# One transpose or two for the queries and keys of a pair of blocks

## The chip, the cores and the metric

The kernel runs on one core of a Trainium2 chip. A core has five engines that run side by side: TensorE for matrix products (PE in the profile; the loading of its weights is listed apart as PEld), VectorE (DVE), ScalarE (ACT), GpSimd (POOL) and SyncE (SP). SP computes nothing here: it issues the transfers, one after another in the order of the program, and 16 DMA engines carry them out. The metric is the time of one execution on the device, in microseconds (us). Three executions of the kernel before took 1917.46, 1920.43 and 1922.58 us, so the median is 1920.43 us.

## The reference

The program is one layer of an encoder block on 2048 positions of width 1024. All of it must come out, in float32:

```python
h = rms_norm(x, norm_gain)
qa, ka, va, qb, kb, vb, ga, gb, mg = split(h @ w_in)          # one combined projection
# mixer A: 8 query heads, 2 key heads, window of 128 positions to each side, a sink logit per head
ya = banded_attention(norm(qa) / 8, norm(ka), va, 128, 1, rel_bias[:, :8], sink_a) * silu(ga)
# mixer B: three groups of 8 heads, (window, dilation) = (128, 1), (512, 4), (2048, 16)
for g: o_g, lse_g = dilated_group(norm(qb_g) / 8, norm(kb_g), vb_g, window_g, dilation_g, bias_g)
yb = sum_g softmax_g(lse)_g * o_g * silu(gb)
out = x + (sigmoid(mg_a) * (ya @ w_branch_a) + sigmoid(mg_b) * (yb @ w_branch_b)) @ w_out
```

The products are made with operands that are split into a high and a low half-precision part, so each float32 product is three half-precision products on TensorE.

## The kernel before, in words

**Stages.** First x is normed, transposed and split (`XH`, `XL`) and a gate is projected. Then come 14 *units*, each a few heads of one mixer: `A` twice and `B` twelve times (four head pairs by three dilations). The first unit is A, the second B with dilation 4, the third A again, and the rest are B. After the units come the merge gates, the branch projections and the output projection, which this change does not touch.

**A unit** walks over 16 blocks of 128 positions, two at a time: a *pair*, eight pairs to a unit. For each block TensorE projects q, k and v into PSUM (`matmuls`, L695). Then, for the whole pair, ACT copies q and k out (`rw`), ACT, DVE and POOL norm and scale them, ACT and DVE write the high and the low part into a tile `spl` (`hi`, L768, and `lo`, L772), and POOL copies the keys once more with the two parts exchanged (`swap`, L777, one copy for each block). `spl` so holds, for each of the two blocks, six strips of 128 columns. In a unit of kind A five heads are normed together for each block (four query heads and one key head, plus the exchanged key); in kind B four (two and two, plus two exchanged).

**The transposes.** The scores need q and k with the head's elements on the partitions, so SP issues a DMA transpose from `spl` into a tile `kq` (`turn`, L785). Before, that is one transpose per block, six strips of 128 by 128, into a tile of its own. There are six such tiles used in turn, and three more (`kq0`) for block 0 of units of kind B that need it again at their end.

**An item** is one block of queries and two heads. An A pair makes four items. Each has score products on TensorE (`logits`, L845, which read `kq`), a minimum with the bias on DVE (L860), exponentials on ACT (L868), the split into `p` (ACT L873, DVE L877), a DMA transpose of `p` into `pt` (`turn` of the item, L883), and the products with v on TensorE (`values`, L894, which read `pt`). In an A unit a `pt` transpose moves twelve strips of 128 by 128 (eight at the unit's ends). The four `pt` tiles are used in turn.

**What sets the order.** The program's order on each engine is written out by hand: each step of a pair or item is put into a heap with a time in units of a pair's length (`NORM`, `LAGS`, `LV`), and the heap is emptied in order of that time between TensorE's products. The times only set an order. On the chip an instruction starts when its engine reaches it and the semaphores that it waits for have come. SP therefore carries, in one queue, the `kq` and `pt` transposes, the loads of weights (`wraw`, L176), biases (`b`, L669) and gate values (`yo`, L944), and the stores (`ytd`, L975, and `zd`, L929).

Of the kernel before, what the change touches and what calls it, by code (L numbers as in the profile page):

```python
# [22 lines left out]
F16 = mybir.dt.float16  # L23
# [9 lines left out]
NT = S // 128  # L33
# [63 lines left out]
X_US = dict(look=0.25, land=4.3, next=1.45, late=.12, sq=1.14, st=.17, ln=.2, nw=.75, sc=1.24, tr=.8, hi=.5, lo=.62, gs=2.1, pw=1.3,  # L97
            gh=1.06, gl=1.26, mm=.217, th=.6, gt=.63, us=.83, uh=.75, ul=.82, ag=1.0, tl=1.3)
XT_BUFS = 14
KQ_BUFS = 6  # L100
VT_BUFS = 10
PT_BUFS = 4
N_BIAS_A = 384
# [3 lines left out]
def block_kernel(tc, x, w_units, w_gate, w_mrg, w_out, w_bra, w_brk, gain, qkg, sink, bias_a, bias_b, b_merge, out):  # L107
    nc = tc.nc
    V = nc.vector
    A = nc.scalar  # L110
# [511 lines left out]
    wk = main.enter_context(tc.tile_pool(name="wk", bufs=2, reuse_waits="tile"))  # L622
# [55 lines left out]
    class Pair:  # L678
# [98 lines left out]
                G.tensor_copy(sp[:, i, nh:, :, :], sp[:, i, nq:nh, ::-1, :])  # L777

        def turn(self):
            for i, s in enumerate(self.subsets):  # L780
                if self.un.shift and s[1] == 0:
                    kq = wk.tile([128, 6, 128], F16, name="kq0", bufs=3)
                else:
                    kq = wk.tile([128, 6, 128], F16, name="kq", bufs=KQ_BUFS)
                nc.sync.dma_start_transpose(out=kq[:], in_=self.sp[:, i].rearrange("p a b c -> p (a b c)"))  # L785
                self.un.kq[s] = kq


    class Item:
# [1215 lines left out]
    outs = [Out(s) for s in range(8)]  # L2005
# [14 lines left out]
    for s in range(8):  # L2020
        p = pos[0]
# [92 lines left out]
```

## Time and profile before

| | |
|---|---|
| median of 3 executions | 1920.43 us |
| the profiled execution | 1923.34 us, of which the span of its instructions is 1920.9 us |
| TensorE busy | 1876.6 us, 98% of the span |
| VectorE busy | 1501.5 us, 78% |
| ScalarE busy | 1251.2 us, 65% |
| DMA transposes | 224 of `kq`, 256 of `pt`, all issued by SP |
| granted TensorE clock, mean | 0.998 |

A row of the waits reads: the engine and line that waited, what it waited for, the sum of the waits, how many, and the longest. In a timeline a row gives start, duration, engine, line, operation, tiles written and read, count, and in brackets the idle time just ahead of it with what ended it. A row of windows gives the stretch, its length, the busy time of each engine with its count of instructions, the granted clock, the share of the DMA engines' time and the bytes moved. SP's rows are the time that the issuing takes; the packets of a transfer move later.

In the profiled execution the first unit A has its pairs between some 95 and 231 us, the second between some 288 and 425 us.

### The profile page before, as it was taken

Reading aid. Unit: us, or ns where it says so; the run is one execution under the profiler, and the core shown is the slowest. Engines: PE = TensorE matmul, PEld = TensorE weight load, DVE = VectorE, ACT = ScalarE, POOL = GpSimd, SP = SyncE. Lnnn points to the kernel's source line nnn. Section 1 sums busy time; section 2 is a strip of 40 time slices with the busy share of each in tenths; the row PEclk is TensorE's granted clock in tenths of the full one; section 3 lists DMA queues with packets and bytes.
Section 4 is the critical chain, followed back from the end, with each engine's and each line's share of the span. In section 5 each row is a group of like instructions: output and inputs, shape, how many; then the busy total and the mean of one; then the engine's idle time right before and its main releaser. Section 6 shows DMA issues by size and latency. Waiting matters only on the chain.

```text
span 1920.9 us, 51094 instructions
## 1 busy us (share of the span) xinstructions
PE 1876.6 (98%) x19242; PEld 1439.4 (75%) x19242; DVE 1501.5 (78%) x3835; ACT 1251.2 (65%) x3015; POOL 579.1 (30%) x1363
## 2 busy tenths in 40 slices
PE   6999999999999999999999999999999999899998
PEld 4568987789999899988999898544444446676774
DVE  7679878986887889878789888657778644977885
ACT  8477768887777777777767766575675865433441
POOL 1034333443553435543455445200000001222121
PEclk9999999999999999999999999999999999999999
DMA  6259998988888679887888777776576557854551
GB/s 255 83 98 197 165 183 143 190 169 165 166 150 182 138 156 202 153 157 175 146 169 160 137 148 146 180 295 181 182 214 181 183 186 252 270 153 120 148 153 61
DMA packets 639351, 326.21 MB, mean 170 GB/s; under 512 B 459264, under 2 KB 589952, under 8 KB 636672
## 3 DMA queue, kind: packets, MB, share of 16 engines
q1 hardware_dynamic: 638960, 322.70, 72.6%
q8 instruction: 150, 2.46, 0.6%
q14 instruction: 97, 0.79, 0.2%
q10 hardware_dynamic: 144, 0.26, 0.0%
HBM read 139.08 MB, written 73.66 MB: 111 GB/s over the span
## 4 chain that ended last, share of the span: by engine, by line
PE 86%; DMA 6%; DVE 4%; ACT 2%; issue 1%; SPq 1%; POOL 0%; DVEq 0%; POOLq 0%
PE pj L695 42%; PE fps L1600 17%; PE fps L1984 7%; PE fps L1912 6%; PE s L845 5%; PE pv L894 4%; DMA pt<-p 2%; PE pj L350 2%; PE pj L302 1%; PE fps L302 1%; DMA kq<-spl 1%; DMA bigl<-ytd 1%; PE pt L958 1%; DMA bigl<-sd 1%; PE s L480 0%
## 5 line engine op out<-in xcount | busy, mean ns | idle before, releaser
L695 PE MATMUL pj<-wl,XH 128*128 128x128 f16 (+2 forms) x2816 | 715.9, 268 | 0.0
L695 PE MATMUL pj<-wh,XL 128*128 128x128 f16 (+2 forms) x2816 | 712.2, 269 | 0.0
L695 PE MATMUL pj<-wh,XH 128*128 128x128 f16 (+2 forms) x2816 | 709.4, 268 | 0.0
L695 PEld LDWEIGHTS <-XH 128*128 128x128 f16 x5632 | 575.4, 112 | 54.6
L695 PEld LDWEIGHTS <-XL 128*128 128x128 f16 x2816 | 316.0, 112 | 24.0
L860 DVE CUSTOM_DVE_ANT_0 pr<-s,b,ubuf 128x256 f32<-128x256 f32 (+3 forms) x512 | 218.9, 465 | 42.1 <-PE s L845 39.5
L877 DVE SCALAR_TENSOR_TENSOR p<-pr,p 128x512 f16<-128x512 f32 (+2 forms) x256 | 195.8, 765 | 51.5 <-ACT p L873 48.6
L762 POOL TENSOR_TENSOR rw<-rw,g 128x128 f32<-128x128 f32 (+1 forms) x224 | 149.2, 686 | 202.5 <-DVE rw L755 170.2
L1922 POOL TENSOR_TENSOR g<-g,t 128x512 f32<-128x512 f32 x32 | 48.5, 1515 | 529.5 <-DVE t L1845 529.5
L1600 PEld LDWEIGHTS <-wh 128*128 128x128 f16 x1064 | 104.2, 99 | 123.5 <-issue 0.6
L713 ACT ACTIVATE rw<-pj 128x256 f32<-128x256 f32 (+1 forms) x224 | 87.4, 390 | 130.0 <-PE pj L695 129.3
L777 POOL COPY spl<-spl 128x256 f16<-128x256 f16 (+1 forms) x224 | 96.7, 461 | 244.5 <-DVE spl L772 244.5
L873 ACT ACTIVATE p<-pr 128x512 f16<-128x512 f32 (+2 forms) x256 | 157.7, 616 | 14.6 <-DMA pt<-p 10.3
L1912 PE MATMUL fps<-y,bigh 128*128 128x128 f16 x1792 | 153.8, 219 | 3.9 <-DVE r L1845 3.9
L1984 PE MATMUL fps<-WO,mf 128*128 128x512 f16 x672 | 151.9, 382 | 3.8 <-DVE xr L1991 3.8
L1912 PE MATMUL fps<-y,bigl 128*128 128x128 f16 x896 | 151.8, 219 | 0.0
L845 PE MATMUL s<-kq 128*128 128x128 f16 (+1 forms) x1856 | 148.2, 218 | 3.6 <-DMA kq<-spl 2.7
L1912 PEld LDWEIGHTS <-bigh 128*128 128x128 f16 x1792 | 139.1, 98 | 11.6 <-issue 4.3
L845 PEld LDWEIGHTS <-kq 128*128 128x128 f16 x2016 | 130.9, 98 | 19.9 <-issue 4.5
L894 PE MATMUL pv<-vt,pt 128*128 128x65 f16 (+1 forms) x2784 | 131.9, 193 | 8.1 <-DMA pt<-p 7.4
L894 PEld LDWEIGHTS <-pt 128*128 128x128 f16 x3024 | 119.3, 98 | 24.1 <-DMA pt<-p 12.1
L768 ACT ACTIVATE spl<-rw 128x512 f16<-128x512 f32 (+1 forms) x112 | 72.0, 643 | 80.3 <-POOL vt L724 70.2
(252 smaller groups left out, 3816.7 us busy)
## 6 DMA issues: line engine op xcount, KB each, us to landing
wraw<-in_w_units_dram SPq DMA_DIRECT2D x56, 384.0 KB, 4.8
g<-mgd SPq DMA_DIRECT2D x64, 256.0 KB, 4.9
wraw<-in_w_mrg_dram SPq DMA_DIRECT2D x45, 256.0 KB, 4.2
mgd<-t SPq DMA_DIRECT2D x43, 256.0 KB, 2.9
zd<-z SPq DMA_DIRECT2D x128, 66.0 KB, 2.0
zz<-zd SPq DMA_DIRECT2D x64, 132.0 KB, 3.4
xt<-in_x_dram SPq DMA_DIRECT2D x16, 512.0 KB, 8.2
ytd<-yo SPq DMA_DIRECT2D x32, 256.0 KB, 3.3
```

The source lines that it names most:

```text
L695: out.append(lambda lhs=lhs, rhs=rhs, ch=ch, a=a, b=b, k=k: T.matmul(ps[:, a:b], lhsT=lhs[:, ch, :], rhs=rhs[:, ch, a:b], start=(k == 0), ...
L713: A.activation(self.rw[:, n * i:n * i + n], self.ps[i][:, :n], AF.Copy)
L762: G.tensor_tensor(q[:, i, :un.nq, :], q[:, i, :un.nq, :], g, OP.mult)
L777: G.tensor_copy(sp[:, i, nh:, :, :], sp[:, i, nq:nh, ::-1, :])
L845: T.matmul(self.sv[j][:, o:o + k1 - k0], lhsT=q[:, h, :], rhs=kt[:, un.nq + kh + v * un.nk, k0:k1], start=(v == 0), stop=(v == 1))
L860: V.tensor_tensor_reduce(out=self.pv[:, j, self.p0:self.p0 + W], in0=self.sv[j], in1=un.bias[:, self.h0 + j, self.b0:self.b0 + W], scale=I ...
L873: A.activation(self.sp[:, :128 * n], self.pr, AF.Copy, scale=PSC)
L877: V.scalar_tensor_tensor(self.sp[:, 128 * n:], self.pr, PSC, self.sp[:, :128 * n], OP.mult, OP.subtract)
L894: T.matmul(self.po[:, j, :w], lhsT=p[:, n * j + s, :], rhs=un.v[key][:, vh, c0:c0 + w], start=(k == 0 and s == 0), stop=(k == 2 and s == n ...
L1600: T.matmul(b[k][:], lhsT=w[:, i, ch, :], rhs=xform(PROD[i][0], lo, ch, q), start=(i < 3 and n == 0), stop=(n == 11), skip_group_check=True)
L1912: out.append(lambda p=p, c=c, wl=wl, yl=yl, n=n: T.matmul(ps[:, 128 * p:128 * p + 128], lhsT=w[wl][:, i, c, p, :], rhs=y[:, yl, c, :], sta ...
L1984: out.append(lambda p=p, ml=ml, wl=wl, k=k: T.matmul(ps[:], lhsT=m[:, ml, p, :], rhs=WO[:, i, wl, p, :], start=(fresh and k == 0), stop=(k ...
```

## The change

For units of kind A the two blocks of a pair are transposed by one DMA transpose of twelve strips into one pair tile of `[128, 12, 128]`. For units of kind B there are still two transposes of six strips, now into the two halves of a pair tile. Four pair tiles are used in turn, in the place of six block tiles. `kq0` stays only for block 0 of a B unit of 16 blocks in a row (dilation 1), in one tile in the place of three; with dilation 4 block 0 stays in its pair tile. The room is the same: nine blocks' worth of tiles before and after.

```diff
@@ -97,7 +97,7 @@
 XT_BUFS = 14
-KQ_BUFS = 6
+KQ_BUFS = 4
 VT_BUFS = 10
@@ -777,13 +777,16 @@
         def turn(self):
+            kq = wk.tile([128, 12, 128], F16, name="kq", bufs=KQ_BUFS)
+            outs = [kq[:, 6 * i:6 * i + 6] for i in range(2)]
+            if self.un.shift and self.un.n == NT and self.subsets[0][1] == 0:
+                outs[0] = wk.tile([128, 6, 128], F16, name="kq0", bufs=1)[:]
+            if self.un.kind == "A":
+                nc.sync.dma_start_transpose(out=kq[:], in_=self.sp[:].rearrange("p s a b c -> p (s a b c)"))
             for i, s in enumerate(self.subsets):
-                if self.un.shift and s[1] == 0:
-                    kq = wk.tile([128, 6, 128], F16, name="kq0", bufs=3)
-                else:
-                    kq = wk.tile([128, 6, 128], F16, name="kq", bufs=KQ_BUFS)
-                nc.sync.dma_start_transpose(out=kq[:], in_=self.sp[:, i].rearrange("p a b c -> p (a b c)"))
-                self.un.kq[s] = kq
+                if self.un.kind == "B":
+                    nc.sync.dma_start_transpose(out=outs[i], in_=self.sp[:, i].rearrange("p a b c -> p (a b c)"))
+                self.un.kq[s] = outs[i]
```

Every line after the function stands three lines lower in the changed kernel: L845 becomes L848, L883 becomes L886.

The order of the instructions on TensorE, VectorE, ScalarE and GpSimd is the same, instruction by instruction. On SP 16 transposes are gone, one for each of the 16 pairs of the two A units, and nothing else has moved past another.

SP's queue in the first unit A, seventh and eighth pair, before. In brackets is what a row waits for: `DMAHW` and a number is the completion of an earlier transfer, `Pool`, `DVE` and `PE` are the engines.

```order
L785 DMA_TRANSPOSE kq<-spl 128x6x128 [waits DMAHW1_49,Pool_49]
L785 DMA_TRANSPOSE kq<-spl 128x6x128 [waits DMAHW2_49,Pool_49]
L944 DMA yo<-gtd_88 128x512 [waits DMAHW3_49]
L883 DMA_TRANSPOSE pt_2417<-p_2357 128x12x128 [waits DMAHW4_49,DVE_49,PE_49]
L975 DMA ytd<-yo 128x512 [waits DMAHW5_49,DVE_49]
L883 DMA_TRANSPOSE pt_2496<-p_2445 128x12x128 [waits DMAHW6_49,DVE_49,PE_49]
L176 DMA wraw<-in_w_units_dram 128x768 [waits DMAHW7_49]
L176 DMA wraw<-in_w_units_dram 128x768 [waits DMAHW0_49]
L883 DMA_TRANSPOSE pt_2581<-p_2533 128x12x128 [waits DMAHW1_49,DVE_49,PE_49]
L883 DMA_TRANSPOSE pt_2664<-p_2616 128x12x128 [waits DMAHW2_49,DVE_49,PE_49]
L785 DMA_TRANSPOSE kq<-spl 128x6x128 [waits DMAHW3_49,Pool_49]
L785 DMA_TRANSPOSE kq<-spl 128x6x128 [waits DMAHW4_49,Pool_49]
```

The same place in the changed kernel:

```order
L785 DMA_TRANSPOSE kq<-spl 128x12x128 [waits DMAHW3_49,Pool_49]
L947 DMA yo<-gtd_88 128x512 [waits DMAHW4_49]
L886 DMA_TRANSPOSE pt_2403<-p_2345 128x12x128 [waits DMAHW5_49,DVE_49,PE_49]
L978 DMA ytd<-yo 128x512 [waits DMAHW6_49,DVE_49]
L886 DMA_TRANSPOSE pt_2482<-p_2431 128x12x128 [waits DMAHW7_49,DVE_49,PE_49]
L176 DMA wraw<-in_w_units_dram 128x768 [waits DMAHW0_49]
L176 DMA wraw<-in_w_units_dram 128x768 [waits DMAHW1_49]
L886 DMA_TRANSPOSE pt_2567<-p_2519 128x12x128 [waits DMAHW2_49,DVE_49,PE_49]
L886 DMA_TRANSPOSE pt_2650<-p_2602 128x12x128 [waits DMAHW3_49,DVE_49,PE_49]
L785 DMA_TRANSPOSE kq<-spl 128x12x128 [waits DMAHW4_49,Pool_49]
```

Each `pt` transpose and each load behind a pair's q and k stands one transpose nearer to the front. The single transpose waits for POOL's second copy (`swap`) of its pair, where the first of two waited for the first copy alone.

TensorE in the first unit A, before: scores of the item that is the first to read the second block of a pair, the rows where the wait for that block's own transpose stands.

```order
L845 LDWEIGHTS kq
L845 MATMUL s<-kq 128x128 [waits DMAHW2_49]
L845 LDWEIGHTS kq
L845 MATMUL s<-kq 128x128
L845 LDWEIGHTS kq
L845 MATMUL s<-kq 128x128 [waits DVE_49]
```

The same rows in the changed kernel:

```order
L848 LDWEIGHTS kq
L848 MATMUL s<-kq 128x128
L848 LDWEIGHTS kq
L848 MATMUL s<-kq 128x128
L848 LDWEIGHTS kq
L848 MATMUL s<-kq 128x128 [waits DVE_49]
```

The wait for the second block has gone; the item before, the first to read the pair's first block, waits for the one transpose that brings both. In the units of kind B the waits for `kq` and for its tiles to come free are for the same instructions as before.

## The prediction

> **What bounds the kernel.** I read the page's first lines and its chain of waits first.
>
> ```profile
> span 1920.9 us, 51094 instructions
> PE 1876.6 (98%) x19242; PEld 1439.4 (75%) x19242; DVE 1501.5 (78%) x3835; ACT 1251.2 (65%) x3015; POOL 579.1 (30%) x1363
> ...
> PE 86%; DMA 6%; DVE 4%; ACT 2%; issue 1%; SPq 1%; POOL 0%; DVEq 0%; POOLq 0%
> ```
>
> TensorE is busy 98% of the span and the change takes no work from it. What can be won is idle time of TensorE, and only where a transfer in the two A units ends that idle time. So the second view is that of windows: the steady part of the first and of the second A unit, then all B units behind them, then two stretches for the clock, then four for the transfers.
>
> ```profile
> 134.00:231.00 97.00, 90.84 (x1349) 80.10 (x1345) 84.64 (x220) 76.62 (x182) 36.30 (x80) 0.98 1.04 185
> 308.00:425.00 117.00, 114.82 (x1410) 95.27 (x1407) 107.32 (x279) 101.07 (x244) 49.64 (x103) 1.00 0.94 170
> 425.00:1230.00 805.00, 802.28 (x9720) 739.74 (x9719) 666.63 (x2016) 572.22 (x1601) 370.58 (x991) 1.00 0.82 161
> 202.00:204.00 2.00, 2.00 (x26) 1.73 (x26) 1.21 (x4) 1.80 (x4) 0.00 (x0) 0.54 1.19 266
> 204.00:206.00 2.00, 2.00 (x14) 1.45 (x12) 0.76 (x3) 1.98 (x6) 0.00 (x0) 0.61 0.74 147
> ...
> 176.00:179.90 3.90, 3.90 (x63) 3.89 (x61) 3.73 (x16) 3.06 (x6) 1.43 (x2) 1.00 1.17 285
> 179.90:181.50 1.60, 0.73 (x8) 0.47 (x5) 1.60 (x3) 0.08 (x1) 1.43 (x1) 1.00 1.37 51
> 199.60:201.60 2.00, 0.16 (x3) 0.00 (x0) 1.04 (x4) 0.42 (x2) 0.85 (x5) 1.00 1.35 84
> 341.50:343.00 1.50, 1.30 (x16) 0.85 (x14) 1.36 (x4) 0.63 (x2) 0.86 (x1) 1.00 1.47 32
> ```
>
> TensorE idles 97.0 - 90.84 = 6.2 us in the first A unit, 117.0 - 114.82 = 2.2 us in the second, and 2.7 us in 805 us of B. In A the DMA engines' share is 0.94 to 1.04 (over 1 is possible, packets overlap): they have hardly any room. The last three rows show transfers that nearly stop for 1.5 to 2 us (32 to 84 GB/s, against 285 GB/s just before). The third view is TensorE's timeline at its waits:
>
> ```profile
> 141.36 0.32 PE L894 MATMUL pv<-vt,pt 128*128 128x65 f16 x5 [0.73 <-DMA pt<-p]
> 182.71 0.35 PE L894 MATMUL pv<-vt,pt 128*128 128x65 f16 x6 [2.08 <-DMA pt<-p]
> 196.42 0.36 PE L894 MATMUL pv<-vt,pt 128*128 128x65 f16 x6 [0.36 <-DMA pt<-p]
> 201.90 0.38 PE L894 MATMUL pv<-vt,pt 128*128 128x65 f16 x7 [2.14 <-DMA pt<-p]
> 343.56 0.32 PE L894 MATMUL pv<-vt,pt 128*128 128x65 f16 x5 [0.76 <-DMA pt<-p]
> 373.84 0.30 PE L894 MATMUL pv<-vt,pt 128*128 128x65 f16 x4 [0.56 <-DMA pt<-p]
> 384.39 0.29 PE L894 MATMUL pv<-vt,pt 128*128 128x65 f16 x4 [0.76 <-DMA pt<-p]
> ...
> PE s L845 <- DMA kq<-spl: 2.7, 3, 1.6
> ```
>
> All seven wait for a `pt` transpose, together 7.4 us. The last row is from the waits behind 425 us: TensorE's only three waits for `kq` are there, in B; none is in A. The waits at 182.71, 201.90 and 343.56 come just behind one of the dead stretches. The fourth view says why `pt` is late: SP's own timeline, with DVE's last step on the `p` that is wanted.
>
> ```profile
> 171.52 0.96 DVE L877 SCALAR_TENSOR_TENSOR p<-pr,p 128x768 f16<-128x768 f32 x1 [0.19 <-ACT p L873]
> 187.64 0.96 DVE L877 SCALAR_TENSOR_TENSOR p<-pr,p 128x768 f16<-128x768 f32 x1 [0.19 <-ACT p L873]
> ...
> 172.44 3.13 SPq L785 DMA_TRANSPOSE kq<-spl  x2
> 175.62 0.57 SPq L944 DMA_DIRECT2D yo<-gtd  x1
> 176.30 2.24 SPq L883 DMA_TRANSPOSE pt<-p  x1
> 178.64 0.53 SPq L975 DMA_DIRECT2D ytd<-yo  x1
> 179.27 2.81 SPq L883 DMA_TRANSPOSE pt<-p  x1
> 182.14 1.05 SPq L176 DMA_DIRECT2D wraw<-in_w_units_dram  x2
> 183.30 5.41 SPq L883 DMA_TRANSPOSE pt<-p  x2
> 188.80 3.41 SPq L785 DMA_TRANSPOSE kq<-spl  x2
> 192.31 1.45 SPq L883 DMA_TRANSPOSE pt<-p  x1
> ```
>
> The `p` done at 172.48 is issued at 176.30, that done at 188.60 at 192.31: 3.8 and 3.7 us late, behind a pair's two `kq`. From 172.4 to 194 SP is never free. In this stretch the single queue of SP is what TensorE waits for.
>
> **What goes.** 16 transposes of six strips, eight in each A unit, all on SP. The price is in the views of the two tiles: all `kq`, and two `pt` of twelve strips from the steady part of A.
>
> ```profile
> L785 SPq DMA_TRANSPOSE kq<-spl x224: 1209/1239/3556, 99.1 to 1206.3; - x112
> ...
> L883 SPq DMA_TRANSPOSE pt<-p x2: 1416/1430/1443, 212.7 to 215.6; - x2
> DMA to landing us min/median/max: 3.6/4.0/4.4
> ...
> L785 SPq DMA_TRANSPOSE kq<-spl x4: 1211/1234/1321, 99.1 to 108.6; - x4
> DMA to landing us min/median/max: 2.7/2.8/2.8
> ```
>
> No transpose of q and k with twelve strips exists yet; the nearest row is `pt` with twelve strips, the same shape. Two issues of 1.24 us and the 0.1 us between them become one of 1.43: SP saves 1.1 us in each pair, 16 x 1.1 = 18 us of its queue in all. The packets stay as many. Landing is 2.8 us behind the issue for six strips in a quiet place and 3.6 to 4.0 (least, median) for twelve, so six more strips take 0.8 to 1.2 us to move. Before, the packets of the next transfer could start 2 x 1.34 = 2.7 us behind those of the first half, for so far apart are the issues. Now they start when twelve strips have gone, 1.6 to 2.4 us behind the same point. So a `pt` behind a pair gains 1.1 to 0.3 us; I take 0.8, nearer to the quiet row, since the median holds a transfer that met others. Where the DMA engines are full it is as low as zero, since SP's issues there are held up by the engines themselves (2.24 and 2.81 us in the timeline, where 1.43 is the free price).
>
> **What it is worth on TensorE.** Four waits stand in a stretch where the engines keep up between the dead stretches: 141.36, 343.56, 373.84 and 384.39. At 0.8 us each they are covered: 0.73 + 0.76 + 0.56 + 0.76 = 2.8 us. The other three are in the full stretch. If the shift gets through, the one at 182.71 loses 0.8, the one at 196.42 all 0.36, and the one at 201.90, behind two merged pairs, 1.6: 2.8 us. If not, 0. I take half, 1.4. The idle time just before 201.9 is followed by two windows with the clock at 0.54 and 0.61, which cost 2 x 0.46 + 2 x 0.39 = 1.7 us; whether they go with the wait is open between 0 and 1.7, I take half, 0.85. The Trainium skill ("TensorE: Matmul & The Clock Gate", Part 1) says that the clock is either full or half and falls to half after an idle window of some 3.4 us; the trace agrees, a fall right behind the stretch with 0.16 us of work in 2.0. By that rule the whole 1.7 us goes or stays, and half is only its expectation.
>
> **What else the edit touches.** A pair's first block now lands with the second: 0.8 us later than alone in a quiet place. Cover: TensorE reads it first in the next item. The tightest place is the pair at 172.44:
>
> ```profile
> L785 SPq DMA_TRANSPOSE kq<-spl x2: 1283/1518/1754, 172.4 to 174.3; - x2
> DMA to landing us min/median/max: 4.3/4.9/5.5
> ...
> 179.14 0.22 PE L845 MATMUL s<-kq 128*128 128x128 f16 x1
> ```
>
> The first half landed at 172.44 + 5.5 = 177.9, the second at 174.3 + 4.3 = 178.6, the use is at 179.1. Even at the second's old time the single transpose is 0.5 us early, and its issue is over sooner. Elsewhere it would have to be later than that. The extra wait for POOL's second copy costs at most the 0.3 us by which the copies are apart, and from the fourth pair on nothing: here POOL ended them at 169.5.
>
> ```profile
> 168.33 1.19 POOL L777 COPY spl<-spl 128x128 f16<-128x128 f16 x2 [3.67 <-DVE spl L772]
> ```
>
> TensorE has one wait fewer per pair; I price it at nothing, since it never stood idle there. The kinds B keep their transposes and the instructions that free the tiles, so nothing is priced there; the 2.7 us of idle time in B bound a gain.
>
> **Sum.** 2.8 + 1.4 + 0.85 = 5.1 us. The profiled execution took 1923.3 us (span 1920.9, 2.4 around it), so it becomes 1918.2; the median of the three executions lies 2.9 us under the profiled one, and on that footing I predict 1915.3 us. The bounds of the terms are 2.8 us, nothing through the full stretch, and 2.8 + 2.8 + 1.7 = 7.3 us, everything.
>
> **Rivals.**
> (a) Everything goes through: SP's lateness, 3.8 us, is a sum over two pairs, and each dead stretch hits a transfer that TensorE wants later. Then the waits are nearly gone, 7.4 us, and the clock's 1.7 with them: 9.1 us, 1911.3. For it speaks that `p` lay ready for 3.7 us; against it that the engines' share is already 1.04.
> (b) The transfers are the limit and SP's issue is hidden: the DMA engines carry the same bytes, their share stays, and `pt` lands when it did. Then 0 to 1 us, 1920. The skill says of issuing ("DMA: Bandwidth & Descriptors", Issuing engines are not separate DMA queues) that the time to initiate a DMA "is usually small relative to the DMA itself". By that nothing would be won. The trace differs in size: 1.24 us of issue against 2.8 to landing.
> (c) Slower: the single transpose is caught as a whole. A dead stretch of 1.5 to 2 us that falls on its twelve strips delays the first block too, which before had often landed by then. The price in one pair is that delay less the slack: 2.0 + 0.8 - 1.2 = 1.6 us of idle TensorE, with the clock 3.3. It decides from four such pairs on, if the engines are full and nothing is won besides: 4 x 1.6 = 6.4, so 1926.8. For it: the slack of 1.2 us at 172.44. Against it: in the other pairs of A no wait for `kq` at all.
>
> **How the numbers follow.** The forecast has a chance of 0.59, rival (a) 0.16, (b) 0.14, (c) 0.11. About 0.3%, 5.8 us, is what a measurement of this kernel can tell from no change, so faster means under 1914.7 and slower over 1926.2. The forecast's own range, from the bounds 2.8 and 7.3, is 1913.1 to 1917.6, and lies across the bound: I put 0.28 of it under 1914.7 and 0.31 over. Faster: 0.28 + 0.16 = 0.44. Same: 0.31 + 0.14 = 0.45. Slower: 0.11. The range reaches from (a) with a spread of one us to just over (b), with the spread of the three executions (2 us up): 1910.3 to 1922.4.
>
> **What would show it.** In the changed profile SP's A stretches hold one issue of some 1.4 us for a pair's q and k. The `pt` transpose behind it starts 1.1 us sooner after the pair's first issue. The windows of the A units show less idle time on TensorE, about 4 us of 8.4 gone, and the stretch around 203 a clock near 1.0. No row of L848 in A waits for `kq`. The forecast is wrong if the idle time in A is as before though SP is early (then (b)), or if L848 waits for `kq` there (then (c)). A change of more than 2 us behind 425 us would be something that I have not seen.

## The result

The changed kernel takes 1915.35 us, the median of 22 executions (1910.68 to 1922.52); the kernel before takes 1920.26 us beside it, also over 22 (1915.94 to 1923.60). The ratio is 0.9978 with a 95% interval from 0.9970 to 0.9985: 4.9 us by the medians, 0.22% faster. The interval excludes no change, though the gain is smaller than the 0.3% that the prediction took as the least that can be told from no change. The profiled execution took 1915.24 us, against 1923.34 us before. These 8.1 us overstate the change, as the windows show. This is the page of the changed kernel:

```profile
span 1913.1 us, 51064 instructions
PE 1872.5 (98%) x19242; PEld 1438.5 (75%) x19242; DVE 1502.7 (79%) x3835; ACT 1250.6 (65%) x3015; POOL 578.9 (30%) x1363
...
PE 87%; DMA 5%; DVE 4%; ACT 1%; issue 1%; POOL 0%; SPq 0%; DVEq 0%; POOLq 0%
```

TensorE's work is what it was. In the chain that sets the end, DMA has fallen from 6% to 5% and the share of SP's queue from 1% to 0. The same windows as in the prediction (steady part of the first and second A unit, all B units, and the stretch behind the low clock), changed kernel:

```profile
134.00:231.00 97.00, 91.73 (x1379) 82.39 (x1376) 87.95 (x229) 78.50 (x188) 37.23 (x81) 1.00 1.06 188
308.00:425.00 117.00, 116.26 (x1405) 97.29 (x1402) 108.90 (x283) 100.18 (x244) 51.35 (x101) 1.00 0.95 172
425.00:1230.00 805.00, 800.99 (x9697) 737.00 (x9696) 665.04 (x2016) 571.73 (x1598) 367.73 (x989) 1.00 0.82 160
202.00:204.00 2.00, 2.00 (x39) 1.99 (x38) 1.96 (x6) 1.38 (x6) 0.00 (x0) 1.00 0.87 170
204.00:206.00 2.00, 2.00 (x38) 2.00 (x37) 2.00 (x5) 1.92 (x6) 0.03 (x1) 1.00 0.71 146
```

TensorE idles 97.0 - 91.73 = 5.3 us in the first unit and 117.0 - 116.26 = 0.7 us in the second, 6.0 in all where it was 8.4. The first unit's clock is 1.00 where it was 0.98, worth 0.02 x 97 = 1.9 us. Together 4.3 us, close to the gain of the medians, 4.9 us; a second profile of the changed kernel, shown with the experiments, gives 8.4 - 3.9 + 1.9 = 6.4 us. B idles 4.0 us, 1.3 more than before. Most of the rest of the profiled difference is not from A: in one stretch of the tail, which the edit does not touch, the clock was low before and is not now (kernel before, then changed kernel):

```profile
1660.00:1690.00 30.00, 27.04 (x327) 20.37 (x326) 24.83 (x45) 14.04 (x27) 6.27 (x5) 0.94 0.60 178
```

```profile
1660.00:1690.00 30.00, 28.46 (x358) 22.08 (x357) 25.71 (x44) 11.48 (x22) 7.32 (x5) 1.00 0.55 162
```

That is 0.06 x 30 = 1.8 us of clock and 1.4 us of idle time. With 4.3 from A and 1.3 lost in B these windows explain 6.2 of the 7.8 us between the two spans. This stretch has 0.94 in some of the other kernels' profiles below and 1.00 in others, so it is part of the scatter of single executions. SP's queue at the seventh and eighth pair of the first unit, changed kernel:

```profile
171.67 2.36 SPq L785 DMA_TRANSPOSE kq<-spl  x1
174.08 0.86 SPq L947 DMA_DIRECT2D yo<-gtd  x1
175.05 1.42 SPq L886 DMA_TRANSPOSE pt<-p  x1
...
186.78 1.47 SPq L785 DMA_TRANSPOSE kq<-spl  x1
188.35 2.89 SPq L886 DMA_TRANSPOSE pt<-p  x1
```

From the first issue for q and k to the `pt` behind, the seventh pair takes 175.05 - 171.67 = 3.38 us (3.86 before), the eighth 188.35 - 186.78 = 1.57 (3.51 before). Over the eleven pairs from the fourth of the first unit and the third of the second on, the median of this distance is 1.91 us, where it was 3.09. What TensorE still waits for in the A units (the sum over both from the view of waits, then three rows of its timeline), and in B the waits for `kq`:

```profile
PE pv L897 <- DMA pt<-p: 5.5, 5, 2.3
```

```profile
180.81 0.71 PE L897 MATMUL pv<-vt,pt 128*128 128x65 f16 x18 [1.42 <-DMA pt<-p]
199.57 0.71 PE L897 MATMUL pv<-vt,pt 128*128 128x65 f16 x18 [2.28 <-DMA pt<-p]
224.94 0.53 PE L897 MATMUL pv<-vt,pt 128*128 128x65 f16 x12 [1.11 <-DMA pt<-p]
```

```profile
PE s L848 <- DMA kq<-spl: 3.9, 3, 1.4
```

Seven waits of 7.4 us for `pt` have become five of 5.5. No wait for `kq` has come into A.

### The profile page after: what moved, and what is told of

Read it like the earlier page. It is cut to its first block, busy times and chain, and to the rows that moved or that the text cites. A ratio compares the mean times of both kernels' runs of the same rounds, so it can differ in the third digit from the quotient of the medians.

```text
span 1913.1 us, 51064 instructions
## 1 busy us (share of the span) xinstructions
PE 1872.5 (98%) x19242; PEld 1438.5 (75%) x19242; DVE 1502.7 (79%) x3835; ACT 1250.6 (65%) x3015; POOL 578.9 (30%) x1363
## 4 chain that ended last, share of the span: by engine, by line
PE 87%; DMA 5%; DVE 4%; ACT 1%; issue 1%; POOL 0%; SPq 0%; DVEq 0%; POOLq 0%
PE pj L695 42%; PE fps L1603 17%; PE fps L1987 7%; PE fps L1915 6%; PE s L848 5%; PE pv L897 4%; DMA pt<-p 2%; PE pj L350 2%; DMA kq<-spl 2%; PE pj L302 1%; PE fps L302 1%; PE pt L961 1%; DVE y L1764 1%; DMA bigl<-sd 1%; PE s L480 0%
## 5 line engine op out<-in xcount | busy, mean ns | idle before, releaser
L848 PE MATMUL s<-kq 128*128 128x128 f16 (+1 forms) x1984 | 151.2, 217 | 4.9 <-DMA kq<-spl 3.9
L848 PEld LDWEIGHTS <-kq 128*128 128x128 f16 x2016 | 131.0, 98 | 21.4 <-issue 6.0
L1915 PEld LDWEIGHTS <-bigh 128*128 128x128 f16 x1792 | 139.0, 98 | 10.5 <-issue 3.2
```

The source lines that it names most:

```text
L848: T.matmul(self.sv[j][:, o:o + k1 - k0], lhsT=q[:, h, :], rhs=kt[:, un.nq + kh + v * un.nk, k0:k1], start=(v == 0), stop=(v == 1))
L1915: out.append(lambda p=p, c=c, wl=wl, yl=yl, n=n: T.matmul(ps[:, 128 * p:128 * p + 128], lhsT=w[wl][:, i, c, p, :], rhs=y[:, yl, c, :], sta ...
```

## The experiments

The theory: in the A pairs SP's queue, in order, is late; one issue less lets each `pt` start about 1 us sooner, and TensorE waits less for it. The rivals: the new tiles and rings do it (four pair tiles for six block tiles); it is special to q and k (how they land, the wait that TensorE no longer has); or the DMA engines pay a price for each transfer that the larger one pays once. Each ratio is to the kernel before on the same chip (its medians there: 1920.18, 1917.79 and 1918.23 us).

**Two transposes again, new tiles kept.**

```diff
-            if self.un.kind == "A":
+            if False:
...
-                if self.un.kind == "B":
+                if True:
```

> The changed kernel with its pair tiles, its four buffers and its single kq0, but with two transposes for each pair of kind A as before. Theory (SP's issue time is what was won): all of the gain goes, 1920 us, within 1.5 us of the kernel before; the late issue of pt behind a pair (3.8 us at the seventh pair of the first A unit) is back, and so is the half clock near 203 us, if the wait ahead of it is. Rival (the tiles: four pairs in turn instead of six blocks, waits at release): stays at 1915.

Measured: 1920.5 us, ratio 0.9995 (0.9984 to 1.0005). By the middle values three quarters of the gain are gone (0.0017 of 0.0022), and the interval just touches that of the changed kernel, so the tiles are at most a small part of its cause. The median distance from a pair's q and k to the `pt` behind is back at 3.07 us. The half clock that was expected back near 203 us did not come there (1.00 from 202 to 206 us), though the first unit's mean is 0.98 again.

**The single transpose kept, but one of the pair's four `pt` transposes cut in two.**

```diff
-            nc.sync.dma_start_transpose(out=pt, in_=self.sp)
+            if self.un.kind == "A" and self.i % 2 and self.h0 == 0:
+                nc.sync.dma_start_transpose(out=pt[:, :n, :], in_=self.sp[:, :128 * n])
+                nc.sync.dma_start_transpose(out=pt[:, n:, :], in_=self.sp[:, 128 * n:])
+            else:
+                nc.sync.dma_start_transpose(out=pt, in_=self.sp)
```

> The changed kernel with one merged q/k transpose for each pair, but the pt transpose of one of the four items of a pair is cut into two halves (high part, low part), 16 in all: as many transposes in the A units as before, the same bytes, the q/k part as changed. Theory (it is the number of issues on SP in an A pair that counts, whichever tile they are for): the gain goes, 1919 to 1921 us. Rival (the gain lies in q and k themselves, one landing and one wait of TensorE fewer): stays at 1915 to 1916.

Measured: 1921.43 us, ratio 1.0013 (1.0004 to 1.0023). The count of issues in a pair is that of before, on another tile, and the gain is gone, and a little more. So it is not special to q and k.

**Three transfers of 4 bytes behind each single transpose.** This puts time into SP's queue with next to no bytes.

```diff
+    tinyd = dr.tile([64, 1], F32, name="tinyd")
+    tiny = [0]
...
                 nc.sync.dma_start_transpose(out=kq[:], in_=self.sp[:].rearrange("p s a b c -> p (s a b c)"))
+                for _ in range(3):
+                    tiny[0] += 1
+                    nc.sync.dma_start(out=tinyd[tiny[0] - 1:tiny[0], :], in_=nsnk[0:1, 0:1])
```

> The changed kernel with three transfers of 4 bytes each from SP behind each merged transpose of an A unit: some 1.2 us of issuing by SP put back in each pair, the DMA engines spared. Theory (SP's issue time): the gain goes, 0.9995 to 1.001 of the kernel before. Rival (the DMA engines' own price for a second transpose is what was saved): the gain stays, 0.998.

Measured: 1921.05 us, ratio 1.0007 (0.9998 to 1.0016), against 0.9982 (0.9972 to 0.9992) for the changed kernel in the same comparison, which was run again beside it:

> The changed kernel once more, on the chip of the runs beside it, since the chips differ by 2 us. 0.9978 of the kernel before, as measured first; between 0.997 and 0.9985.

It took 1915.16 us, so the tiny transfers cost 5.9 us. SP's queue at the eighth pair with them:

```profile
189.58 1.47 SPq L787 DMA_TRANSPOSE kq<-spl  x1
191.10 1.95 SPq L790 DMA_DIRECT2D tinyd<-nsnk  x3
193.16 1.44 SPq L891 DMA_TRANSPOSE pt<-p  x1
```

From q and k to `pt` it takes 193.16 - 189.58 = 3.58 us, as before the change (3.51); the median over the same eleven pairs is 3.18 (3.09 before, 1.91 without the tiny transfers). Over all 48 the median issue is 0.25 us:

```profile
L790 SPq DMA_DIRECT2D tinyd<-nsnk x48: 221/250/947, 100.6 to 381.8; - x48
```

TensorE's waits for `pt` in the two A units, tiny transfers:

```profile
PE pv L902 <- DMA pt<-p: 10.2, 8, 2.7
```

The delay of the `pt` issue is back to within 0.1 us of what it was, and the waits for `pt` are back and longer (10.2 us, 5.5 without, 7.4 before). A tiny transfer is a transfer too, so this run alone does not exclude a price for each transfer on the DMA engines. Such a price would lengthen the way of the `pt` transposes from issue to landing. In the window of the first A unit that way is, in the kernel before and in the changed kernel:

```profile
DMA to landing us min/median/max: 3.1/4.7/7.3
```

```profile
DMA to landing us min/median/max: 3.1/4.5/7.1
```

In the second unit, from 308 to 400 us, the medians are 4.3 and 4.2, and with two transposes and the new tiles 4.6 and 4.4 in the two units. The way changes by 0.1 to 0.2 us, while the issue comes 1.2 us sooner. So a price on the DMA engines is small beside SP's time, if there is one; with the tiny transfers the view gives no landing.

The three kernels that give the gain back, the one that gives part, and the changed kernel's second run, by windows of the A units (in this order: two transposes, `pt` cut, tiny transfers, only the first unit merged as below, the changed kernel again):

```profile
134.00:231.00 97.00, 91.17 (x1360) 82.29 (x1359) 85.95 (x224) 77.16 (x185) 36.05 (x79) 0.98 1.05 186
308.00:425.00 117.00, 113.87 (x1396) 94.71 (x1394) 106.41 (x276) 100.70 (x243) 49.71 (x100) 1.00 0.95 169
```

```profile
134.00:231.00 97.00, 90.42 (x1342) 80.84 (x1339) 85.10 (x220) 76.71 (x183) 37.60 (x80) 0.98 1.02 185
308.00:425.00 117.00, 114.82 (x1411) 95.41 (x1410) 108.27 (x280) 101.28 (x243) 48.77 (x103) 1.00 0.98 170
```

```profile
134.00:231.00 97.00, 90.12 (x1329) 80.56 (x1326) 83.27 (x214) 75.22 (x178) 35.29 (x77) 0.96 1.01 182
308.00:425.00 117.00, 113.83 (x1411) 94.41 (x1409) 106.94 (x275) 100.57 (x240) 48.53 (x99) 1.00 0.92 168
```

```profile
134.00:231.00 97.00, 93.78 (x1394) 85.31 (x1393) 88.73 (x232) 78.44 (x187) 38.68 (x81) 0.98 1.07 190
308.00:425.00 117.00, 114.36 (x1381) 95.67 (x1380) 106.91 (x276) 98.38 (x239) 51.33 (x101) 1.00 0.94 171
```

```profile
134.00:231.00 97.00, 93.78 (x1427) 85.40 (x1425) 89.80 (x233) 79.50 (x190) 38.66 (x82) 1.00 1.04 189
308.00:425.00 117.00, 116.34 (x1382) 97.92 (x1381) 107.42 (x281) 99.83 (x248) 52.23 (x107) 1.00 0.94 177
```

TensorE's idle time in these two windows, with what a clock under 1.00 costs there (its shortfall times 97 us), stands beside the ratios thus:

| kernel | idle, first + second (us) | clock (us) | ratio |
|---|---|---|---|
| before | 6.2 + 2.2 | 1.9 | 1 |
| two transposes, new tiles | 5.8 + 3.1 | 1.9 | 0.9995 |
| `pt` cut in two | 6.6 + 2.2 | 1.9 | 1.0013 |
| tiny transfers | 6.9 + 3.2 | 3.9 | 1.0007 |
| first unit merged | 3.2 + 2.6 | 1.9 | 0.9985 |
| changed kernel | 5.3 + 0.7 | 0 | 0.9978 |
| changed kernel again | 3.2 + 0.7 | 0 | 0.9982 |

Each row is one profile. The profiled executions with the tiny transfers (1927.99 us) and with two transposes (1923.92) were the slowest of their kernels, that of the changed kernel again (1912.56) the fastest. Still, with the two numbers added up, the kernels with an extra issue in each pair or its time on SP all stand at 10.3 us or more, the two profiles of the changed kernel at 6.0 or less, and the half merge at 7.7 between them. The second unit shows it most steadily: 0.7 us of idle time with the merge, 2.2 to 3.2 without. Five more profiles, of the runs with the merge in B and with gate values later below, have the merge in both A units: their second unit idles 0.4 to 1.0 us, and their sums are 5.7 to 7.9.

**The merge in the first A unit alone.**

```diff
-            if self.un.kind == "A":
+            if self.un.u == 0:
...
-                if self.un.kind == "B":
+                if self.un.u != 0:
```

> The changed kernel with the merged transpose in the first A unit alone; the second A unit has two per pair. Theory: most is won where SP never gets free and where the clock fell, in the first unit: 1916.5 us, and the second unit's share is what is missing to 1915.4, some 1 us. Rival (the gain is spread evenly, a fixed price for each transpose): half the gain, 1918.

Measured: 1916.02 us, ratio 0.9985 (0.9976 to 0.9994). By the middle values two thirds of the gain are in the first unit; the intervals allow a good deal either way. The second unit idles 2.6 us again.

**The merge in B too.** Everywhere but in the first pair of B units with dilation 1; then with dilation 4 and 16 alone (run in two comparisons); then with dilation 1 alone.

```diff
+            one = not (self.un.shift and self.un.n == NT and self.subsets[0][1] == 0)
...
+            one = self.un.kind == "A" or self.un.d > 1
...
+            one = self.un.d == 1 and (self.un.kind == "A" or self.subsets[0][1] > 0)
```

> The changed kernel with merged transposes in the B units too, except for the first pair of units of dilation 1, whose block 0 has a tile of its own: 92 transposes fewer than in the changed kernel. Theory (SP's time counts only where TensorE waits for what SP issues late): TensorE idles 2.7 to 4 us in all of the B units, so between 1912.5 and 1916 us, likeliest 1915. Rival (each transpose saved is worth a fixed 0.3 us, 5 us over 16): 92 x 0.3 = 28 us less, 1887. Other rival (a B item needs the first block early, and the merged one lands 0.8 us later): 1917 or more, with TensorE's waits at L850 for kq grown in B.

> The changed kernel with merged transposes in B units of dilation 4 and 16 too (64 transposes fewer), dilation 1 as changed. All seven waits of TensorE for kq in the run that merged everywhere stand in units of dilation 1, where q and k are issued behind the loads of zz. Theory (a merged pair costs where its first block is wanted soon and transfers lie ahead of it): no loss here, 1914.5 to 1916.5 us. Rival (a merged pair in any B unit lands too late): half to three quarters of that run's 8.5 us over the changed kernel, 1920 to 1922.

> Merged transposes in A and in B units of dilation 4 and 16, again, beside the changed kernel on the same chip. The profile of the first run has the A units as short as the changed kernel's and only 2 us more in B, so I expect 0 to 2 us more than the changed kernel here, 0.998 to 0.999 of the kernel before. Rival (a merged pair costs in any B unit): 4 us or more over it, 1.000 or more.

> The changed kernel with merged transposes in B units of dilation 1 alone (28 fewer, without each unit's first pair). Theory: most of the 8.5 us loss, 1920 to 1923 us, with TensorE's waits for kq behind 425 us at 6 us or more. Rival: a quarter of it, 1917.

Measured: everywhere 1923.86 us, ratio 1.0018 (1.0007 to 1.0028); dilation 4 and 16 1918.96 us, 1.0008 (0.9997 to 1.0018), and in the comparison with the changed kernel 1918.04 us, 0.9996 (0.9986 to 1.0006); dilation 1 1920.98 us, 1.0018 (1.0007 to 1.0029). Merging everywhere (1915 expected) and the first run of dilation 4 and 16 (1914.5 to 1916.5 expected) missed, on the slow side; the second run of dilation 4 and 16 lies between its expectation and its rival, and dilation 1 alone came as expected. Fewer issues won nothing in B, and with dilation 1 the merge costs. For dilation 1 the view of waits behind 425 us shows a part of why (merged everywhere, then dilation 1 alone, then dilation 4 and 16):

```profile
PE s L849 <- DMA kq<-spl: 8.2, 7, 2.1
```

```profile
PE s L849 <- DMA kq<-spl: 7.5, 7, 1.7
```

```profile
PE s L849 <- DMA kq<-spl: 4.5, 3, 2.7
```

With dilation 1 merged TensorE waits for `kq` twice as long as in the changed kernel (3.9 us); the ten profiles with two transposes in B have 2.7 to 5.6 us. The 4 us more are about half of the loss, 0.0040 x 1918 = 7.7 us against the changed kernel; the other half is not explained. One such place, SP's queue and TensorE's wait, merged everywhere:

```profile
494.58 1.18 SPq L907 DMA_DIRECT2D zz<-zd  x2
496.19 5.38 SPq L786 DMA_TRANSPOSE kq<-spl  x1
...
503.81 0.50 PE L849 MATMUL s<-kq 128*128 128x128 f16 x6 [1.75 <-DMA kq<-spl]
```

The issue stands behind two loads of `zz` and takes 5.38 us there, the transpose lands 7.6 us behind its start, and both blocks of the pair land late together: this is the prediction's rival of the transpose that is caught as a whole, in another unit. Transfers nearly stop twice within that landing (8 to 21 GB/s), and the share of the loads and of the stops was not separated. With dilation 4 and 16 the waits, 4.5 us, lie within the scatter of the profiles with two transposes, and the loss against the changed kernel is 0.14% (2.9 us) beside it. Its cause stays open.

**SP relieved in another way: plain transfers issued by ScalarE**: loads of weights for two units, of gate values, and the stores of `ytd`. The same edit was made on the kernel before and on the changed kernel.

```diff
-            nc.sync.dma_start(out=raw[:, 2 * i:2 * i + 2, :n], in_=src[:, 2 * i:2 * i + 2, :])
+            (nc.scalar if u in (1, 3) else nc.sync).dma_start(out=raw[:, 2 * i:2 * i + 2, :n], in_=src[:, 2 * i:2 * i + 2, :])
...
-            nc.sync.dma_start(out=self.o[:], in_=gtd[self.chunk][:, 512 * self.q:512 * self.q + 512])
+            nc.scalar.dma_start(out=self.o[:], in_=gtd[self.chunk][:, 512 * self.q:512 * self.q + 512])
...
-            nc.sync.dma_start(out=ytd[self.chunk, :, 512 * self.q:512 * self.q + 512], in_=self.o[:])
+            (nc.scalar if self.chunk < 4 else nc.sync).dma_start(out=ytd[self.chunk, :, 512 * self.q:512 * self.q + 512], in_=self.o[:])
```

> The kernel before with its two transposes per pair, but with 32 plain transfers of the A units (gate values in, gated results out, weights of the units behind them) issued by ScalarE and not by SP. As many transfers, the same bytes, less work for SP: some 10 us of issuing in the first A unit and 6 in the second. Theory (SP's issue time is what makes pt late): a gain without any merging, 1915 to 1918 us. Rival (the DMA engines' own cost for each transfer is what the merging saves): 1920, no change. Other rival: ScalarE, 80% busy in these units and now waiting for the stores' data and the loads' tiles, gets late itself: 1922 or more.

> The changed kernel with the same 32 transfers on ScalarE. Theory: what is left of TensorE's waits for pt in the A units, 5.5 us in the profile, shrinks by a further 1 to 3 us: 1912.5 to 1914.5 us. Rival (the DMA engines are full and set what is left): 1915.4, as the changed kernel. Rival ScalarE late: 1917 or more.

Measured: 1924.78 us, ratio 1.0035 (1.0021 to 1.0048), and 1921.59 us, 1.0023 (1.0011 to 1.0035). Both expectations missed, on the other side, where they had put a ScalarE that gets late itself. No wait of TensorE between 95 and 425 us is put down to ScalarE in either profile; that it delays others on the way is not excluded. SP's queue at the seventh pair, the landing of that `kq` and of the `pt` behind it, the waits from 95 to 425 us (the two A units and the B unit between them), and the transfers from 170 to 184 us by queue (packets, MB, share), all of the changed kernel with this edit:

```profile
170.36 1.62 SPq L785 DMA_TRANSPOSE kq<-spl  x1
172.16 4.73 SPq L886 DMA_TRANSPOSE pt<-p  x1
```

```profile
DMA to landing us min/median/max: 10.5/10.5/10.5
```

```profile
DMA to landing us min/median/max: 9.8/9.8/9.8
```

```profile
PE s L848 <- DMA kq<-spl: 5.4, 2, 3.6
PE pv L897 <- DMA pt<-p: 3.2, 6, 1.1
```

```profile
q1 hardware_dynamic: 6102, 2.43, 98.0%
q10 hardware_dynamic: 288, 0.52, 16.7%
```

SP is early now, and `pt` is issued 1.80 us behind the start of q and k (3.38 without the edit). But `kq` lands 10.5 us behind its issue, where it took 5.3 in the changed kernel, and TensorE waits 3.6 us for it. The waits for `pt` shrink (3.2 us for 5.5) and those for `kq` take their place; of the two, that of 3.6 us is in A and the other in the B unit. In the kernel before with the same edit the waits for `pt` do not shrink (8.2 us, 7.4 without), and one of 2.4 us for `kq` is new in that B unit. So it is not shown that relieving SP without a merge wins time: with these loads and stores on another queue the kernel got slower. ScalarE's queue (q10) moves 0.52 MB beside SP's stream there. That the transposes are slowed by the plain transfers that now run beside them fits these rows; one of the stops told of at the end lies within that landing too, and the two were not separated. The Trainium skill ("DMA: Bandwidth & Descriptors", Issuing engines are not separate DMA queues) says that transfers started by ScalarE, SP or GpSimd run on the same 16 DMA engines and interleave. These longer landings fit that, and do not prove it.

**Gate values loaded later.** SP's `yo` load moved out from between the pair's q and k and its `pt`:

```diff
-Y_PART = (-0.02, 0.571, 0.797, 0.981, 1.031)
+Y_PART = (0.2, 0.571, 0.797, 0.981, 1.031)
```

> The changed kernel with the loads of gate values in the first A unit issued later, behind one more pt transpose instead of right behind a pair's q and k. In the changed profile two of TensorE's largest waits (1.4 and 2.3 us) are for a pt that stands right behind such a load. Theory (what stands ahead of pt on SP counts): 1 to 2.5 us less than the changed kernel, 0.9965 to 0.9975 of the kernel before. Rival (the full DMA engines set these waits, or the gate now waits for its values): as the changed kernel, 0.998, or more.

Measured: 1916.89 us, ratio 0.9985 (0.9975 to 0.9996), within the intervals of the changed kernel: a miss, nothing is won. In its profile, the slowest of its executions, the two waits that were aimed at have shrunk from 1.42 and 2.28 us to 0.59 and 0.44, but one of 2.94 us is new at 211.65, behind another stretch in which the transfers nearly stop. None of these versions beat the changed kernel.

## Why the prediction was right

The forecast, 1915.3 us, was met by the median of 1915.35, and its mechanism stands: SP's time in the A pairs, and TensorE's waits for `pt`. By its steps:

- **The price of an issue: right.** 1.43 us was taken from the `pt` transposes. The sixteen single transposes measure 1.42 at least and 1.51 in the median, in stretches where the engines are busier:

```profile
L785 SPq DMA_TRANSPOSE kq<-spl x16: 1424/1514/2364, 99.0 to 372.1; - x16
```

- **`pt` 1.1 us sooner in each pair: right in the middle, uneven in size.** Over the eleven pairs the median is 1.2 us. It was 0.5 us at the seventh pair, where the single issue itself took 2.36 us, and 1.9 at the eighth.
- **The four waits outside the full stretch, 2.8 us: nearly right, but a new one came.** Those at 141.36 and 343.56 have no successor; in the second unit 2.1 us of `pt` waits became 0.7 (one of 0.53 is left at 379.58). But a new one of 1.11 us stands at 224.94 (0.48 in the second profile). The prediction counts 343.56 as a place where the engines keep up, though its own table has it right behind a dead stretch. The changed kernel's transfers nearly stop there too (4 to 10 GB/s up to 339.1 us), and TensorE idles only 0.05 us from 338 to 340. So a dead stretch need not cost TensorE time when the issue is earlier.
- **Half of 2.8 us in the full stretch: 0.9 in one profile, 2.2 in the other.** In the first, the middle wait, 0.36, has gone; 2.08 became 1.42, and 2.14 became 2.28. In the second profile of the changed kernel the two that are left are 1.48 and 0.89 us, at 179.25 and 196.24, and all waits for `pt` in A are

```profile
PE pv L897 <- DMA pt<-p: 3.4, 4, 1.5
```

  In the first profile the two come right behind a stretch in which the transfers nearly stop, as before:

```profile
178.50:179.70 1.20, 0.89 (x11) 0.62 (x8) 1.16 (x4) 0.35 (x1) 0.75 (x1) 1.00 0.06 6
197.80:199.20 1.40, 0.00 (x0) 0.00 (x0) 0.36 (x2) 0.00 (x0) 0.70 (x5) 1.00 0.48 20
```

- **The clock, 0.85 as an expectation: it went whole** in this profile, 1.7 us (1.00 and 1.00 for 0.54 and 0.61), though the wait just ahead of it stayed. The first unit's clock is 1.00 in both profiles of the changed kernel and in three of the five others that merge both A units, 0.98 in two of them and with the merge in the first unit alone, and 0.98 or 0.96 where SP's time was put back. The prediction says that the trace agrees with a fall behind some 3.4 us of idle time. The half clock is there (0.50 from 203 to 205 us before), but the idle time ahead of it was 2.14 us, and in the changed kernel 2.28 us were followed by 1.00: how much idle time it takes, these traces do not show.
- **No wait for `kq` in A: right.** At the seventh pair it landed at 171.67 + 5.3 = 177.0, before the 177.9 and 178.6 of the two.
- **About 4 of 8.4 us of idle time gone in A: 2.4 in the first profile, 4.5 in the second** (3.2 + 0.7 us left).
- **Nothing over 2 us behind 425: right for B** (1.3 us more idle time), while the tail's low-clock stretch above shows that a single profile can differ by more there.
- **The rival that transfers are the limit and SP's issue is hidden fell**: three ways of putting the issue's time back gave the gain back. Some 1.2 us of SP's queue in each of 16 pairs were worth 0.0017 x 1920 = 3 us (two transposes) to 5.9 us (tiny transfers), 0.2 to 0.3 of each microsecond. The Trainium skill ("DMA: Bandwidth & Descriptors", Issuing engines are not separate DMA queues) says of the time to start a transfer that it "is usually small relative to the DMA itself"; that would mislead here. The slower rival did not happen in A; a transpose caught as a whole was seen in B with dilation 1 when the merge was put there. That everything goes (1911.3) fell too, by the two waits that stayed.

Added up like the prediction's terms, the first profile gives 2.1 - 1.1 + 0.9 + 1.7 = 3.6 us (the four waits, the new one, the full stretch, the clock) and the second 2.3 - 0.5 + 2.2 + 1.7 = 5.7, where the sum was 5.1 and the medians moved by 4.9. The mechanism and the size of the whole are borne out, the single terms only roughly, and a single profile cannot settle them. That the median lay within 0.1 us of the forecast is luck beside the scatter of single executions, 12 us.

## What to carry to other kernels

Where TensorE waits for a transfer, look at the issuing queue's own timeline: if the data lay ready for some us before the issue, one instruction less ahead of it is worth a part of its issue time, and here a transposing transfer of twice the size cost little more to issue than a small one (1.51 us for 1.24). Merge only where that queue is late and the first half has slack; behind the loads of `zz` the merge made both halves late. Moving other transfers to a second queue is not the same as removing an issue: here it freed SP's queue, `kq` landed later at the place shown, and the kernel got slower.

## What was not expected of the hardware

**Stretches in which transfers nearly stop move with the program.** Before they stood at 179.9 and 199.6, now at 178.5 and 197.8, at 6 and 20 GB/s. In the transfers of the first of them in the changed kernel (177 to 181 us; kind, packets, MB, share) a packet of a queue of the kind `instruction` stands beside the data's:

```profile
q1 hardware_dynamic: 1983, 0.78, 119.5%
q8 instruction: 1, 0.02, 1.8%
```

This is a coincidence seen at several places, before and after; that this packet stops the transposes was not tested.

**The clock falls in different places from execution to execution.** The 30 us of the tail shown above have 0.94 in the profile before, 1.00 after, 1.00 with `pt` cut, and 0.94 with two transposes and with the tiny transfers: 1.8 us each time. What decides it stays open.
